# Eight of the weight sums of a down projection: accumulating DMA, or a plain load and an add on GpSimd

## The chip, the cores and the metric

The kernel runs on one core of one Trainium2 chip. The metric is the device time of one execution in microseconds. Before the change it is 768.64 us, the median of three runs (767.77 to 768.9).

## The reference

One layer of a hybrid decoder: 512 tokens of width 1024 go through a state-space mixer and an attention mixer, an output projection, and then a gated MLP with a short convolution. All is float32. What matters here is the last product of the MLP, with D_FF = 2816:

```python
def conv_gated_mlp(x, w_up, conv_w, conv_b, w_down):
    h = x @ w_up.astype(x.dtype)
    h = causal_depthwise_conv(h, conv_w, conv_b)
    gate, val = jnp.split(h, 2, axis=-1)
    return (jax.nn.silu(gate) * val) @ w_down.astype(x.dtype)
...
        hf = rms_norm(x, norm_ffn_w[layer])
        x = x + conv_gated_mlp(hf, w_up[layer], ffn_conv_w[layer], ffn_conv_b[layer], w_down[layer]).astype(x.dtype)
```

## The kernel before

Float32 products are made of three matmuls each: both operands are split into a high part (a cast on ScalarE, `wh`, `oh`) and a low part (the rest, a subtraction on VectorE, `wl`, `ol`), and high x high, high x low and low x high are summed in PSUM (`mm3`, L110).

The down projection is the last stage, from about 650 us on. It cuts the tokens, the inner dimension and the output columns in halves and needs seven products instead of eight (`PRODUCTS`, n = 0 to 6). Their left operands are quarters or sums of quarters of the activations, their right operands quarters of `w_down` or sums of them:

- products 0 and 1 use the quarters B11 and B21 as they are, loaded by SP into `wraw` (`load_unit`);
- products 2, 3, 4 use a running sum T: B11 + B12, then B22 added, then B21 added;
- products 5 and 6 use T again, loaded afresh with B22, then B12 added.

Each quarter has 11 blocks of 128 rows, and a product walks through them in six units of two blocks (1024 columns; the sixth has one block, 512). T[u] is the sum for unit u: six tiles. Where a row names tiles, T[0] and T[1] are both printed as `T`, T[2] to T[5] in the order lists as `T_7091` to `T_7094`.

A unit of a product is worked on so: ScalarE casts T[u] to `wh`, VectorE forms `wl` (both L1218, `split_unit`), TensorE runs 12 matmuls of 512 columns (6 in the last unit). There are three buffers for `wh` and `wl`, so a split can run at most three units ahead of TensorE. In the same loop `next_sum(n, u)` starts the next term of T[u], `SUMS` lets VectorE make sums of activations (L1413, L1419), `split_into` splits the next left operand (L1354 on ScalarE, L1355 on VectorE), and at the end of a product VectorE adds its PSUM banks to the output in SBUF (L1514, one input in PSUM).

The terms of T come by two kinds of DMA. `fresh` (L1200) is a plain load, issued by SP. `gather` (L1207) is a load that adds to what the tile holds, issued by GpSimd. `next_sum` calls them: in product 1, units 4 and 5, for T[2] to T[5] (B11 fresh, then B12 gathered); in products 2, 3 and 5 one gather per unit, as soon as the unit's `wl` has been made; in product 4 one fresh load per unit. T[0] and T[1] get their first two terms before the stage.

The order on ScalarE and VectorE is pinned by the order of the code (`in_turn`); SP and GpSimd work through their queues in the order that the scheduler gives them, and an instruction that waits holds all behind it. At L1155 and L1156, in the up stage, GpSimd has two multiplications of 512 columns per step, placed behind a chosen instruction of VectorE (`in_shadow`).

Of the kernel before, what the change touches and what calls it, by code (L numbers as in the profile page):

```python
# [8 lines left out]
F32 = mybir.dt.float32  # L9
# [6 lines left out]
P = 128  # L16
# [23 lines left out]
def tile_hybrid_layer(  # L40
# [18 lines left out]
    nc = tc.nc  # L59
    act, dve, pool, pe = nc.scalar, nc.vector, nc.gpsimd, nc.tensor  # L60
# [165 lines left out]
    for k in range(NK):  # L226
        ins = pe.matmul(pdt[:64, :], wdt[:, k, :], xh[:, k, :], start=k == 0, stop=False, skip_group_check=True)
        if k < 2:
            tc.keep_in_program_order(ins)
            keep_busy(64 * (1 - k))  # L230
        ins = pe.matmul(
            pdt[:32, :], wdt[:, k, 0:32], xl[:, k, :], start=False, stop=k == NK - 1, skip_group_check=True
        )
# [564 lines left out]
    B11, B12, B21, B22 = 0, 1, 2, 3  # L798
    ADD, SUB = ALU.add, ALU.subtract
# [32 lines left out]
    turn_of = {}  # L832
# [359 lines left out]
    UNITS = [(k, min(k + 2, NH)) for k in range(0, NH, 2)]  # L1192

    def part(q, u):
        return wdown[q, :, UNITS[u][0] * 512 : UNITS[u][1] * 512]

    T = []

    def fresh(q, u):
        nc.sync.dma_start(T[u], part(q, u))  # L1200
# [5 lines left out]
    def gather(q, u):  # L1206
        nc.gpsimd.dma_start(T[u], part(q, u), accum_op=ALU.add)  # L1207
# [143 lines left out]
    q = NH - 1  # L1351
# [55 lines left out]
    pt_ = ctx.enter_context(tc.tile_pool(name="pt", bufs=1, side="right", reuse_waits="tile"))  # L1407
# [39 lines left out]

    ADDED = {2: B22, 3: B21, 5: B12}

    def next_sum(n, u):  # L1450
        if n == 4:
            fresh(B22, u)
        if n in ADDED:
            gather(ADDED[n], u)
        if n == 1 and u > 3:
            for v in ((2, 3), (4, 5))[u - 4]:
                fresh(B11, v)
                gather(B12, v)

    ops = [a11]  # L1460

    def units_of(n):
# [8 lines left out]
        for u, (lo, hi) in enumerate(UNITS):  # L1471
            early = n == 0 and u < 3
            if not early:
                h, l = split_unit(u, T[u] if quarter is None else load_unit(quarter, u))
            next_sum(n, u)
            if (n, u) in SUMS:
                add, v = SUMS[n, u]
# [151 lines left out]
```

## Time and profile before

| | us |
|---|---|
| median of three runs | 768.64 |
| the profiled execution's own time | 770.09 |
| its span, first to last instruction | 768.3 |
| TensorE busy | 759.0 |
| VectorE busy | 600.0 |
| ScalarE busy | 489.0 |
| GpSimd busy | 201.0 |

The granted clock of TensorE is 1.000 over the span. The rows of the profile are read so: start or place, busy time, engine (PE is TensorE, DVE VectorE, ACT ScalarE, POOL GpSimd, SPq SyncE's queue), line, operation, tile written <- tiles read, shapes, count; in brackets, how long the engine sat idle before it and who released it. What GpSimd waited for longest in the down stage (engine, line, tile <- releaser: total, times, longest):

```profile
POOL T L1207 <- DVE wl L1218: 26.0, 10, 13.0
POOL T L1207 <- PE X L110: 20.3, 1, 20.3
POOL T L1207 <- DVE x L1514: 8.3, 3, 3.2
```

A wait is put down to the releaser that came last by the profile; where that engine had long been done, it was another, often a DMA.

### The profile page before, as it was taken

How to read it: one execution, taken by the hardware profiler on the slowest of the kernel's cores; microseconds unless marked ns; L12 is line 12 of the kernel's file. 1: busy time of each engine (PE TensorE's matmuls, PEld its weight loads, DVE VectorE, ACT ScalarE, POOL GpSimd, SP SyncE). 2: the span in 40 equal slices, each digit the busy share in tenths (PEclk: the TensorE clock that was granted, in tenths of full speed). 3: DMA queues.
4: the chain of work that ended last, by engine and by line, in shares of the span. 5: the costliest groups of instructions: out<-in, count | busy, mean ns of one | idle time of the engine just before them, and what ended most of it. 6: DMA issues, size and time to landing. Idle time of an engine off the chain costs nothing.

```text
span 768.3 us, 12543 instructions
## 1 busy us (share of the span) xinstructions
PE 759.0 (99%) x4647; PEld 652.2 (85%) x4647; DVE 600.0 (78%) x965; ACT 489.0 (64%) x870; POOL 201.0 (26%) x250
## 2 busy tenths in 40 slices
PE   9999999999999999999999999999999999999997
PEld 7888878888888768887777799999999999887786
DVE  5896788578567675578794887988888888998785
ACT  7655767754578667785673665666666666665461
POOL 0001013443454542314200001333333333223120
PEclk9999999999999999999999999999999999999999
DMA  9534233143155143343222318888888888589983
GB/s 341 175 105 142 84 123 121 57 137 110 57 164 165 43 137 90 116 138 110 83 83 89 106 57 162 195 196 202 195 198 196 189 194 195 144 227 204 241 180 100
DMA packets 35005, 112.39 MB, mean 146 GB/s; under 512 B 4160, under 2 KB 5248, under 8 KB 34944
## 3 DMA queue, kind: packets, MB, share of 16 engines
q1 hardware_dynamic: 24176, 74.89, 28.7%
q0 software_dynamic: 10336, 36.18, 26.2%
q8 instruction: 36, 0.59, 0.3%
q10 hardware_dynamic: 432, 0.52, 0.2%
q14 instruction: 25, 0.20, 0.1%
HBM read 105.71 MB, written 2.20 MB: 140 GB/s over the span
## 4 chain that ended last, share of the span: by engine, by line
PE 92%; issue 3%; DMA 1%; POOL 1%; DVE 1%; ACT 0%; DVEq 0%; POOLq 0%; ACTq 0%
PE G L110 19%; PE pw L110 17%; PE g L110 13%; PE po L110 12%; PE Z L110 10%; PE Y L110 3%; PE o L684 3%; PE X L110 2%; PE pT L674 2%; PE y L501 2%; DMA T<-in_wdown_dram 1%; PE j L110 1%; PE S L652 1%; PE S L651 1%; POOL T L1207 1%
## 5 line engine op out<-in xcount | busy, mean ns | idle before, releaser
L110 PE MATMUL pw<-wl,xh 128*128 128x512 f32 x192 | 75.9, 395 | 0.0
L110 PE MATMUL pw<-wh,xh 128*128 128x512 f32 x192 | 75.3, 397 | 0.0
L110 PE MATMUL pw<-wh,xl 128*128 128x512 f32 x192 | 75.3, 394 | 0.0
L110 PE MATMUL G<-uh,wh 128*128 128x256 f32 x264 | 72.6, 277 | 0.4 <-ACT wh L923 0.4
L110 PE MATMUL G<-uh,wl 128*128 128x256 f32 x264 | 71.6, 277 | 1.1 <-DVE wl L923 1.1
L110 PE MATMUL G<-ul,wh 128*128 128x256 f32 x264 | 72.5, 276 | 0.0
L97 DVE TENSOR_TENSOR wl<-wraw,wh 128x1024 fp32r<-128x1024 f32 x51 | 63.2, 1241 | 9.3 <-ACT wh L96 9.1
L96 ACT CAST wh<-wraw 128x1024 fp32r<-128x1024 f32 x51 | 53.9, 1056 | 14.7 <-PE g L110 5.3
L110 PE MATMUL g<-xl,wh 128*128 128x512 f32 x144 | 56.7, 394 | 0.0
L110 PE MATMUL g<-xh,wh 128*128 128x512 f32 x144 | 56.5, 393 | 0.0
L110 PE MATMUL g<-xh,wl 128*128 128x512 f32 x144 | 56.5, 393 | 0.0
L968 POOL DMA_DIRECT2D Ta<-in_wup_dram x30 | 26.2, 873 | 113.1 <-DVE wl L923 113.1
L1218 ACT CAST wh<-T 128x1024 fp32r<-128x1024 f32 (+1 forms) x32 | 31.5, 985 | 35.5 <-DMA T<-in_wdown_dram 19.2
L657 ACT ACTIVATE prob<-prob,nm 128x128 f32<-128x128 f32 (+1 forms) x64 | 35.8, 561 | 25.9 <-DVE nm L653 25.8
L923 DVE TENSOR_TENSOR wl<-Ta,wh 128x1024 fp32r<-128x1024 f32 x40 | 48.7, 1218 | 2.6 <-ACT wh L923 2.6
L653 DVE CUSTOM_DVE_ANT_0 prob<-S,prob 128x128 f32<-128x128 f32 (+1 forms) x64 | 30.1, 487 | 26.3 <-PE S L652 23.8
L110 PEld LDWEIGHTS G<-uh,wh 128*128 128x128 f32 x264 | 49.6, 188 | 0.8 <-ACT wh L923 0.8
L110 PEld LDWEIGHTS G<-uh,wl 128*128 128x128 f32 x264 | 48.9, 188 | 1.3 <-DVE wl L923 1.3
L110 PEld LDWEIGHTS G<-ul,wh 128*128 128x128 f32 x264 | 49.6, 188 | 0.0
L1218 DVE TENSOR_TENSOR wl<-T,wh 128x1024 fp32r<-128x1024 f32 (+1 forms) x32 | 36.5, 1139 | 14.8 <-ACT wh L1218 14.6
L923 ACT CAST wh<-Ta 128x1024 fp32r<-128x1024 f32 x40 | 42.1, 1052 | 6.2 <-DMA Ta<-in_wup_dram 4.2
L110 PE MATMUL G<-sh,wh 128*128 128x256 f32 x160 | 44.2, 276 | 0.0
(296 smaller groups left out, 2416.9 us busy)
## 6 DMA issues: line engine op xcount, KB each, us to landing
Ta<-in_wup_dram POOLq DMA_DIRECT2D x30, 512.0 KB, 5.4
T<-in_wdown_dram POOLq DMA_DIRECT2D x20, 512.0 KB, 7.3
wraw<-in_wqk_dram SPq DMA_DIRECT2D x16, 512.0 KB, 3.6
wraw<-in_wout_dram SPq DMA_DIRECT2D x16, 512.0 KB, 3.4
wraw<-in_wup_dram SPq DMA_DIRECT2D x14, 512.0 KB, 4.5
wraw<-in_wxbc_dram SPq DMA_DIRECT2D x11, 512.0 KB, 3.4
Ta<-in_wup_dram SPq DMA_DIRECT2D x10, 512.0 KB, 6.8
Tb<-in_wup_dram SPq DMA_DIRECT2D x10, 512.0 KB, 6.4
```

The lines of the kernel that those rows point to most:

```text
L96: act.copy(h, r)
L97: dve.tensor_tensor(out=l, in0=r, in1=raw(h), op=ALU.subtract)
L110: ins = pe.matmul(o, a, b, start=start and n == 0, stop=stop and n == 2, **kw)
L501: ins = pe.matmul(o[rows, j * P : (j + 1) * P], w[:, h * HD : (h + 1) * HD], m[:, h, :], start=start and j == 0, stop=stop and j == 3, ski ...
L651: pe.matmul(sps[:, :n], qst, ks[:, 0, :n], start=True, stop=False)
L653: dve.tensor_tensor_reduce(out=p, in0=sps[:, :n], in1=p, scale=-1.0, scalar=-NEG, op0=ALU.add, op1=ALU.min, accum_out=nm[:, qb : qb + 1],)
L657: act.activation(p, p, AF.Exp, scale=-1.0, bias=nm[:, qb : qb + 1], accum_out=sm[:, qb : qb + 1])
L674: pe.transpose(t[:, w : w + P], prob[:, o : o + P], ident)
L684: ins = pe.matmul(o[rows, kb * P :], v[:, kb, (2 * pair + i) % 8, :], pt[:, w : w + SEQ - kb * P], start=kb == 0, stop=kb == NTB - 1, skip ...
L923: ordered(act.copy(h, r), lambda: dve.tensor_tensor(out=l, in0=r, in1=raw(h), op=SUB))
L968: last_more[0] = nc.gpsimd.dma_start(t, wup[quarter, q], accum_op=ALU.add)
L1218: ordered(act.copy(hs, src[:, :n]), lambda: dve.tensor_tensor(out=ls, in0=src[:, :n], in1=raw(hs), op=SUB))
```

## The change

Eight of the terms that `gather` brought are now brought by a plain load of SP into a tile of its own (`beside`, four buffers of 1024 columns), and GpSimd adds that tile to T[u] with a `tensor_tensor`. They are B12 for T[3] and T[5] in product 1, and B22 and B21 for T[0], T[2] and T[4] in products 2 and 3. The load is made to wait for the low part that VectorE formed last at that point of the code. The other terms stay gathers.

```diff
     ADDED = {2: B22, 3: B21, 5: B12}
 
+
+    BESIDE_FIRST = (3, 5)
+    BESIDE = (0, 2, 4)
+
+    def add_beside(q, u):
+        w = (UNITS[u][1] - UNITS[u][0]) * 512
+        t = pt_.tile([P, 1024], F32, tag="beside", name="beside", bufs=4)
+        dep = mybir.DependencyInfo(mybir.DependencyClass.Sync, mybir.DependencyReason.DATA)
+        ins = nc.sync.dma_start(t[:, :w], part(q, u))
+        tc.add_manual_dep(ins.ins, turn_of["l"].ins.name, dep, reason="issue_after")
+        pool.tensor_tensor(out=T[u][:, :w], in0=T[u][:, :w], in1=t[:, :w], op=ADD)
+
     def next_sum(n, u):
         if n == 4:
             fresh(B22, u)
-        if n in ADDED:
+        if n in (2, 3) and u in BESIDE:
+            add_beside(ADDED[n], u)
+        elif n in ADDED:
             gather(ADDED[n], u)
         if n == 1 and u > 3:
             for v in ((2, 3), (4, 5))[u - 4]:
                 fresh(B11, v)
-                gather(B12, v)
+                (add_beside if v in BESIDE_FIRST else gather)(B12, v)
```

The instructions of TensorE, VectorE and ScalarE stand in the same order as before. GpSimd's queue, from its last multiplication of the up stage to T[4]'s first gather of the stage and the terms of product 2; before:

```order
L1156 TENSOR_TENSOR KK<-ua 128x512
L1207 DMA T_7091<-in_wdown_dram 128x1024
L1207 DMA T_7092<-in_wdown_dram 128x1024
L1207 DMA T_7093<-in_wdown_dram 128x1024
L1207 DMA T_7094<-in_wdown_dram 128x512
L1207 DMA T<-in_wdown_dram 128x1024 x2
```

and after the change, through product 2's terms:

```order
L1156 TENSOR_TENSOR KK<-ua 128x512
L1207 DMA T_7091<-in_wdown_dram 128x1024
L1207 DMA T_7093<-in_wdown_dram 128x1024
L1460 TENSOR_TENSOR T_7092<-T_7092,beside 128x1024
L1207 DMA T<-in_wdown_dram 128x1024
L1460 TENSOR_TENSOR T_7094<-T_7094,beside 128x512
L1460 TENSOR_TENSOR T<-T,beside 128x1024
L1207 DMA T_7092<-in_wdown_dram 128x1024
L1460 TENSOR_TENSOR T_7091<-T_7091,beside 128x1024
L1207 DMA T_7094<-in_wdown_dram 128x512
L1460 TENSOR_TENSOR T_7093<-T_7093,beside 128x1024
```

T[4]'s gather moved up past T[3]'s term, and gathers and adds now alternate. The rest of the queue goes on so for product 3: the add to T[0], the gathers of T[1] and T[3], the add to T[2], the gather of T[5], the add to T[4].

SP's queue, from the fresh load of T[5] in product 1 to the first fresh load of product 4, as a difference (`out_dram` is the output of product 1):

```order
 L1200 DMA T_7094<-in_wdown_dram 128x512
-L1518 DMA out_dram<-x_85 128x512 x2
+L1458 DMA beside<-in_wdown_dram 128x1024
+L1458 DMA beside<-in_wdown_dram 128x512
+L1458 DMA beside<-in_wdown_dram 128x1024
+L1532 DMA out_dram<-x_85 128x512 x2
+L1458 DMA beside<-in_wdown_dram 128x1024 x5
 L1200 DMA T<-in_wdown_dram 128x1024 x2
```

Three of the new loads (T[3], T[5], and T[0] of product 2) stand ahead of the two stores, five between them and product 4's fresh loads.

## The prediction

> **What bounds the kernel now.** I read the page first, then TensorE's rows in the down stage, then what its waits lead back to.
>
> ```profile
> PE 759.0 (99%) x4647; PEld 652.2 (85%) x4647; DVE 600.0 (78%) x965; ACT 489.0 (64%) x870; POOL 201.0 (26%) x250
> 700.05 0.39 PE L110 MATMUL Y<-wh,oh 128*128 128x512 f32 x1
> 716.24 0.39 PE L110 MATMUL X<-wh,oxh 128*128 128x512 f32 x1
> 733.81 0.39 PE L110 MATMUL Z<-wh,oh 128*128 128x512 f32 x1
> 748.77 0.39 PE L110 MATMUL Y<-wh,oh 128*128 128x512 f32 x1
> ```
>
> TensorE is busy 99% of the span, so only its gaps can be won. The four matmul rows are the first ones of products 3, 4, 5 and 6 of the down stage, each of 66 matmuls. Product 5 takes 748.77 - 733.81 = 14.96 us undisturbed; product 3 takes 16.19 and product 4 takes 17.57. So the two lose 1.23 + 2.61 = **3.8 us**. What ends the largest gap is seen on three engines:
>
> ```profile
> 727.45 1.05 ACT L1218 CAST wh<-T 128x1024 fp32r<-128x1024 f32 x1 [2.30 <-DMA T<-in_wdown_dram]
> 728.53 1.23 DVE L1218 TENSOR_TENSOR wl<-T,wh 128x1024 fp32r<-128x1024 f32 x1 [1.43 <-ACT wh L1218]
> 729.81 0.50 PE L110 MATMUL X<-wl,oxh 128*128 128x512 f32 x1 [0.76 <-DVE wl L1218]
> ```
>
> The sum T lands late, ScalarE casts it, VectorE forms the low part, and TensorE starts at once. Why does T land late? The first row is the DMA view's of 696 to 704 us, the second its of 678 to 682 us (packets, MB, share of the engines); then two of GpSimd's issues, and the first one's time to landing:
>
> ```profile
> q0 software_dynamic: 445, 1.63, 105.6%
> q1 hardware_dynamic: 465, 1.48, 95.3%
> 690.87 0.86 POOL L1207 DMA_DIRECT2D T<-in_wdown_dram x1 [1.59 <-DVE wl L1218]
> 698.48 0.87 POOL L1207 DMA_DIRECT2D T<-in_wdown_dram x1 [1.56 <-DVE ol L1355]
> T<-in_wdown_dram POOLq DMA_DIRECT2D x1, 512.0 KB, 7.3
> ```
>
> Gathers alone fill all 16 DMA engines: 1.63 MB in 8 us, or 2.57 us for one of 0.524 MB; plain loads move 1.48 MB in 4 us, or 1.41 us for one. The gather of 690.87 lands 7.3 us later, at 698.2, and the third one after it is issued 0.3 us behind that, as if no more than three could be under way. So what limits products 3 and 4 is the gathers' DMA time.
>
> **What the change removes.** Eight gathers (7.5 full ones, since unit 5 is half) become plain loads: 7.5 x (2.57 - 1.41) = 8.7 us less DMA time between about 681 and 724 us. The gaps are far smaller than that, so this removes the whole **3.8 us** if nothing else is late. The next candidate on DMA is the gather of T[2] for product 2. Its landing is just in time now:
>
> ```profile
> 688.21 1.05 ACT L1218 CAST wh<-T 128x1024 fp32r<-128x1024 f32 x1 [2.46 <-DMA T<-in_wdown_dram]
> 690.70 0.40 PE L110 MATMUL Z<-wl,oh 128*128 128x512 f32 x1
> ```
>
> From cast to matmul lie 2.49 us, of which 1.05 + 1.23 are the two conversions: 0.2 us to spare. In the changed kernel the plain loads of units 3 and 5 share the engines with this gather, while the gather of T[3] behind it is gone. Bounds: nothing, and the plain loads' whole 1.5 x 1.41 = 2.1 us less the spare, 1.9; I take **0.5 us**, nearer to nothing because a gather of 2.57 us leaves.
>
> **What it adds: SP.** Eight loads in SP's queue, each waiting for the low part of its unit.
>
> ```profile
> T<-in_wdown_dram SPq DMA_DIRECT2D x10, 512.0 KB, 7.0
> ```
>
> Behind the third load stand the two stores of product 1's output, behind the last the fresh loads of product 4; both wait for later work of VectorE than the loads ahead of them do. A load lands in 7.0 us (median of such loads of T), an add takes 2.3, and between a unit's low part and the cast of its next sum lies about one product, 14.96 us. I cost this at nothing; the cover is the 5 us that are left, and each us beyond them would stall TensorE by one.
>
> **What it adds: GpSimd.** Seven adds of 1024 columns and one of 512. The nearest rows:
>
> ```profile
> 620.10 1.29 POOL L1155 TENSOR_TENSOR ua<-ua 128x512 f32<-128x512 f32 x1 [1.75 <-DVE wl L923]
> 621.36 1.29 POOL L1156 TENSOR_TENSOR KK<-ua 128x512 f32<-128x512 f32 x1
> 183.64 1.26 POOL L543 TENSOR_TENSOR yt<-yt 128x256 f32<-128x256 f32 x2
> ```
>
> The first two are 1.26 us apart for 512 columns. The third is a pair of 256 and 128 columns (the loop at L543) in 1.26 us. With a fixed part a and b per column, a + 512b = 2a + 384b = 1.26, so a = 0.25, b = 1.97 ns, and 1024 columns take 2.27 us: 7 x 2.27 + 1.26 = **17.2 us**. GpSimd has the room: its 13 issues between 686 and 724 us take 11.3 us (last row below), and more than half of them go. In its queue T[1]'s gather stands behind T[3]'s add, and later each gather behind one or two adds, so an add that waits for its load holds a gather back. The larger price is elsewhere:
>
> ```profile
> 117.39 1.09 POOL L486 TENSOR_SCALAR_AFFINE_SELECT sc<-sc 128x1024 f32<-128x1024 f32 x1 [7.23 <-ACT ce L484]
> 194.57 1.70 POOL L486 TENSOR_SCALAR_AFFINE_SELECT sc<-sc 128x1024 f32<-128x1024 f32 x1
> 194.11 1.22 DVE L485 TENSOR_TENSOR ce<-ce,cT 128x1024 f32<-128x1024 f32 x1
> 195.24 1.58 DVE L541 TENSOR_TENSOR msl<-y,msh 128x512 fp32r<-128x512 f32 x1
> 656.17 2.36 DVE L1218 TENSOR_TENSOR wl<-wraw,wh 128x1024 fp32r<-128x1024 f32 x2 [0.27 <-ACT wh L1218]
> 657.55 2.15 POOL L1155 TENSOR_TENSOR ua<-ua 128x512 f32<-128x512 f32 x1 [3.59 <-DVE wl L1218]
> 659.66 1.29 POOL L1156 TENSOR_TENSOR KK<-ua 128x512 f32<-128x512 f32 x1
> 660.58 1.45 DVE L1218 TENSOR_TENSOR wl<-wraw,wh 128x1024 fp32r<-128x1024 f32 x1
> 620.34 2.98 DVE L1118 SCALAR_TENSOR_TENSOR ua<-Z,pc,ua 128x511 f32<-128x511 f32 x4 [0.39 <-ACT ua L1111]
> 125.35 0.68 DVE L541 TENSOR_TENSOR msl<-y,msh 128x512 fp32r<-128x512 f32 x1
> 125.96 0.68 DVE L448 SCALAR_TENSOR_TENSOR gz<-th,gz 128x512 f32<-128x512 f32 x1
> 125.38 2.40 POOL L543 TENSOR_TENSOR yt<-yt 128x256 f32<-128x256 f32 x2
> ```
>
> Read in pairs. L486 takes 1.09 us alone, but 1.70 when it meets a VectorE operation with two SBUF inputs: it waits until that ends at 195.3. Then VectorE's L541, 0.68 us elsewhere, takes 1.58: it waits until L486 ends at 196.3. The add at 657.55 likewise takes 2.15, not 1.29, because VectorE's low parts run until 658.5; and the low part at 660.58 takes 1.45, not 1.22, until the add ends at 660.95. So a GpSimd operation and a VectorE operation with two SBUF inputs **exclude each other**, each for the other's whole length. Operations with an input in PSUM show no such stretch: the four at 620.34, beside two adds, take 2.98 us together, and the adds 1.29 each. Who goes first differs: at 195.24 and 660.58 GpSimd went ahead of VectorE's next operation, while at 125.96 VectorE's next one went ahead of the add issued at 125.38 (the pair took 2.40 us, not 1.26). Now VectorE's work in the stretch with the adds, 686 to 724 us:
>
> ```profile
> L1218 DVE TENSOR_TENSOR wl<-T,wh 128x1024 fp32r<-128x1024 f32 (+1 forms) x14 | 16.1, 1148 | 6.0 <-ACT wh L1218 5.9
> L1355 DVE TENSOR_TENSOR ol<-sum,oh 128x512 fp32r<-128x512 f32 (+1 forms) x9 | 5.6, 625 | 0.0
> L1413 DVE TENSOR_TENSOR sum<-sum,KK 128x512 f32<-128x512 f32 (+1 forms) x6 | 3.8, 640 | 0.0
> L1514 DVE TENSOR_TENSOR x<-x,Z 128x512 f32<-128x512 f32 x2 | 1.3, 680 | 0.0
> core 0: us, PE busy (x) PEld busy (x) DVE busy (x) ACT busy (x) POOL busy (x), PEclk, DMA share, GB/s
> 686.00:724.00 38.00, 37.08 (x161) 29.50 (x160) 31.56 (x42) 19.44 (x27) 11.30 (x13) 1.00 1.03 206
> ```
>
> In the last row VectorE's busy time is 31.6 us. All of it has two SBUF inputs except the output adds of L1514, which read PSUM: three pairs of 1.3, less the overlap of starts, 3.7 us. That leaves 27.9 us that must not coincide with the adds. Together 27.9 + 17.2 = 45.1 us. By 724 us TensorE had lost part of its 3.8 us: product 3's 1.23 and the first gap of product 4.
>
> ```profile
> 721.68 0.39 PE L110 MATMUL X<-wh,oxh 128*128 128x512 f32 x1
> 722.45 0.50 PE L110 MATMUL X<-wl,oxh 128*128 128x512 f32 x1 [0.38 <-DVE wl L1218]
> ```
>
> With 14.96 / 66 = 0.23 us from one matmul to the next, this gap is 0.77 - 0.23, and 0.11 more for the stalled matmul's longer row: 0.65. So 1.9 us were lost, and without gaps the same work would be due in 38 - 1.9 = 36.1 us. **45.1 - 36.1 = 9.0 us** too much. VectorE has nothing in hand at the start: T[2]'s low part ends 0.2 us before its matmul. TensorE's queue follows VectorE, so I put these 9.0 us on the path.
>
> I take it that the two alternate, as two of the three places show. [...]
>
> **Sum.** -3.8 + 0.5 + 9.0 = +5.7 us. The profiled execution took 770.09 us (span 768.3), the median is 768.64; on the median this gives **774.3 us**.
>
> **Rivals.**
> *The adds fit in VectorE's pauses.* Its 14 low parts waited 5.9 us for ScalarE, and free time is 36.1 - 27.9 = 8.2 us. If an add held VectorE for less than 8.2 / 17.2 = 48% of its length, nothing would be late and the 3.8 us are won: 764.8 us. For it: the pauses are there. Against it: at 195.24 VectorE's operation can have begun only at 195.24 + 1.58 - 0.68 = 196.14, 0.13 us before L486 ended, so it was held nearly to the end.
> *Both cancel.* If an add held VectorE for about 70% of its length, (8.2 + 3.8) / 17.2, the loss equals the gain: 768.6 us. For it: adds may run beside the six output adds; against it, these are already in the free time.
> *VectorE keeps its turn.* If VectorE's queued operations go first, as at 125.96, an add starts only in a pause, its sum is late, and the gathers that stand behind it in GpSimd's queue are late too, above all T[1]'s gather behind T[0]'s add of product 3. TensorE then waits for sums; VectorE's pauses while it waits are lost. One late gather costs its 7.3 us to landing less the 3 to 4 us that its split runs ahead; once, it adds about 3 us: 777.5 us. For it one row, against it two.
> That the change does not do what it says I leave out: the order lists show the eight loads and adds.
>
> **How the numbers follow.** The forecast gets 0.52, with 2.27 us per add and 0 to 1.9 for T[2] as bounds: 771.5 to 776.5. VectorE first gets 0.26, up to 780. Cancelling gets 0.10, pauses 0.12. The range 766.5 to 779.5 leaves out the pauses' case and the far end of the third. A measurement tells about 0.2%, 1.5 us: faster 0.12, same 0.10, slower 0.78.
>
> **What would show it.** Right: VectorE's low parts (L1218) between 686 and 724 us have means well above 1.15 us, some over 3 us; GpSimd's adds at 2.3 us and up; the casts no longer wait for the DMA; product 2, undisturbed now, loses a few us; products 2 to 4 together lose 8 to 11 us; DMA share falls below 0.9. Wrong: low parts of 1.22 us beside running adds, which would give the first rival; or casts that wait for GpSimd for long while VectorE's rows stay short, which would give the third.

## The result, and the profile after the change

| | before | after |
|---|---|---|
| median, us (four runs of each, side by side) | 768.26 (767.77 to 768.9) | 776.5 (775.08 to 776.88) |
| after / before, 95% interval | | 1.0102 [1.009, 1.0115] |
| the profiled execution's own time | 770.09 | 775.08 |
| its span | 768.3 | 773.3 |
| mean granted clock of TensorE | 1.000 | 0.997 |

The change costs about 1%: 8.2 us between the medians, 7.8 by the ratio. The two profiled executions lie only 5.0 us apart: that of before took longer than any timed run of its kernel, that of after less than the three others. This matters below.

From the page after the change, the busy line, the line of the gathers' queue and the first line of the chain of work that ended last:

```profile
PE 759.4 (98%) x4647; PEld 652.4 (84%) x4647; DVE 612.7 (79%) x965; ACT 489.5 (63%) x870; POOL 218.1 (28%) x250
...
q0 software_dynamic: 9184, 32.25, 23.6%
...
PE 91%; DVE 6%; issue 1%; DMA 0%; ACT 0%; SPq 0%; DVEq 0%; ACTq 0%
```

The gathers' queue moves 32.25 MB where it moved 36.18: the eight terms of 7.5 x 0.524 MB are gone from it. GpSimd is busy 17.1 us longer with as many instructions (eight adds for eight issues of gathers), and VectorE, whose 965 instructions are the same, 12.7 us longer. The chain, which led over the DMA and GpSimd for 1% each, now leads over VectorE for 6%. The shares do not say where that is. The first matmuls of products 2, 3, 4 and 5 of the down stage (TensorE's timeline):

```profile
683.27 0.39 PE L110 MATMUL Z<-wh,oh 128*128 128x512 f32 x1
...
702.97 0.40 PE L110 MATMUL Y<-wh,oh 128*128 128x512 f32 x1
...
722.45 0.39 PE L110 MATMUL X<-wh,oxh 128*128 128x512 f32 x1
...
738.82 0.39 PE L110 MATMUL Z<-wh,oh 128*128 128x512 f32 x1
```

Products 2 to 4 now take 738.82 - 683.27 = 55.55 us. Undisturbed they take 46.05, the stretch from 683.92 to 729.97 us in the run with fills below, where TensorE has no gap: three times 14.96 and the five matmuls of product 1 (5 x 0.23) that stand behind product 2's first one. So they lose 9.50 us: product 2 3.6, product 3 4.5, product 4 1.4. In the profile of before the same stretch, from 683.90 to 733.81, loses 3.86. Where the 9.5 us go, on TensorE's timeline:

```profile
690.95 0.50 PE L110 MATMUL Z<-wl,oh 128*128 128x512 f32 x1 [0.71 <-DVE wl L1218]
...
695.96 0.50 PE L110 MATMUL Z<-wl,oh 128*128 128x512 f32 x1 [1.98 <-DVE wl L1218]
...
711.65 0.80 PE L110 MATMUL Y<-wl,oh 128*128 128x512 f32 x1 [2.73 <-DVE wl L1218]
712.24 0.63 PE L110 MATMUL Y<-wh,ol 128*128 128x512 f32 x1
712.67 0.63 PE L110 MATMUL Y<-wh,oh 128*128 128x512 f32 x1
...
729.39 0.50 PE L110 MATMUL X<-wl,oxh 128*128 128x512 f32 x1 [1.11 <-DVE wl L1218]
```

Every gap is ended by a low part of VectorE. Behind the longest, matmuls follow one another at 0.43 us, not 0.23, until 714.4: about 1.5 of the 9.5 us are a lowered clock (the windows below show 0.66 there). What VectorE does ahead of the gaps, and GpSimd beside it (their timelines):

```profile
687.93 1.83 DVE L1355 TENSOR_TENSOR ol<-sum,oh 128x512 fp32r<-128x512 f32 x1
...
692.50 3.40 DVE L1218 TENSOR_TENSOR wl<-T,wh 128x1024 fp32r<-128x1024 f32 x1
...
704.26 1.21 DVE L1218 TENSOR_TENSOR wl<-T,wh 128x1024 fp32r<-128x1024 f32 x1
...
708.21 3.38 DVE L1218 TENSOR_TENSOR wl<-T,wh 128x1024 fp32r<-128x1024 f32 x1
...
723.78 2.63 DVE L1413 TENSOR_TENSOR sum<-sum,KK 128x256 f32<-128x256 f32 x1
```

```profile
686.81 2.40 POOL L1460 TENSOR_TENSOR T<-T,beside 128x1024 f32<-128x1024 f32 x1 [2.96 <-DMA beside<-in_wdown_dram]
...
690.10 4.73 POOL L1460 TENSOR_TENSOR T<-T,beside 128x512 f32<-128x512 f32 x2
...
703.67 6.84 POOL L1460 TENSOR_TENSOR T<-T,beside 128x1024 f32<-128x1024 f32 x2 [0.74 <-DMA beside<-in_wdown_dram]
```

The low part of 708.21 would take 1.22 us; it takes 3.38, for the pair of adds from 703.67 ends at 710.51 and the low part 1.1 us after that. The sum of 723.78 has 256 columns, 0.42 us elsewhere, and takes 2.63 beside an add from 723.12 to 726.12. An add that begins while VectorE works on PSUM data (686.81) takes 2.40, and that work, the two output adds of 686.74, 1.28 together. Eight VectorE rows of the stretch are so lengthened, one for each add: by 1.15, 1.09, 2.18, 2.21, 1.02, 2.16, 1.21 and 2.21 us, 13.2 us together. The group of low parts in 686 to 724 us (count, then busy time and mean ns, then idle time ahead), and the windows:

```profile
L1218 DVE TENSOR_TENSOR wl<-T,wh 128x1024 fp32r<-128x1024 f32 (+1 forms) x13 | 20.3, 1558 | 1.3 <-ACT wh L1218 1.3
```

```profile
686.00:724.00 38.00, 32.56 (x133) 25.43 (x132) 36.72 (x36) 18.58 (x26) 24.99 (x14) 0.96 0.75 186
...
710.00:715.00 5.00, 3.35 (x9) 2.69 (x10) 5.00 (x6) 0.34 (x1) 1.98 (x3) 0.66 0.59 94
```

VectorE (third busy time) has no pause but 1.3 us, with 36 instructions where it made 42 before; the DMA share is 0.75 where it was 1.03. ScalarE's casts hardly wait for transfers any more (total, times, longest):

```profile
ACT wh L1218 <- DMA T<-in_wdown_dram: 3.2, 2, 2.4
```

Before it was 19.2 us in 12 waits. The relief that the loads bring is there, and the adds take it back and more.

### The profile page after: what moved, and what is told of

Same layout as the page of the kernel before. It is cut to its first block, busy times and chain, and to the rows that moved or that the text cites. A ratio compares the mean times of both kernels' runs of the same rounds, so it can differ in the third digit from the quotient of the medians.

```text
span 773.3 us, 12548 instructions
## 1 busy us (share of the span) xinstructions
PE 759.4 (98%) x4647; PEld 652.4 (84%) x4647; DVE 612.7 (79%) x965; ACT 489.5 (63%) x870; POOL 218.1 (28%) x250
## 3 DMA queue, kind: packets, MB, share of 16 engines
q0 software_dynamic: 9184, 32.25, 23.6%
## 4 chain that ended last, share of the span: by engine, by line
PE 91%; DVE 6%; issue 1%; DMA 0%; ACT 0%; SPq 0%; DVEq 0%; ACTq 0%
PE G L110 19%; PE pw L110 17%; PE g L110 13%; PE po L110 11%; PE Z L110 10%; PE Y L110 4%; PE o L684 3%; DVE wl L1218 2%; PE X L110 2%; PE pT L674 2%; PE y L501 2%; PE j L110 1%; PE S L652 1%; PE S L651 1%; DVE x L1528 1%
## 5 line engine op out<-in xcount | busy, mean ns | idle before, releaser
L1218 DVE TENSOR_TENSOR wl<-T,wh 128x1024 fp32r<-128x1024 f32 (+1 forms) x32 | 41.8, 1306 | 8.2 <-ACT wh L1218 8.2
```

The costliest lines, as they stand in the source:

```text
L1218: ordered(act.copy(hs, src[:, :n]), lambda: dve.tensor_tensor(out=ls, in0=src[:, :n], in1=raw(hs), op=SUB))
```

## The experiments

The theory: an add on GpSimd and an operation of VectorE with two SBUF inputs exclude each other, and VectorE has not enough pauses for the adds. The rivals: the adds make the sums late, or hold the gathers behind them in GpSimd's queue; or the plain loads themselves cost. Each run is timed beside the kernel before on the same chip. The last column is what products 2 to 4 lose in that run's profile, from the first matmul of product 2 to that of product 5 less 46.05 us.

| run | median, us | ratio to before, 95% interval | loss, us |
|---|---|---|---|
| the change again | 776.14 | 1.0091 [1.0076, 1.0107] | 9.0 |
| loads, no adds | 767.28 | 0.9976 [0.9966, 0.9986] | 0.2 |
| fills instead of adds | 766.36 | 0.9975 [0.994, 1.0009] | 0.0 |
| copies instead of adds | 767.23 | 0.9987 [0.9974, 0.9999] | 0.5 |
| adds in halves | 775.49 | 1.0104 [1.0076, 1.0131] | 8.1 |
| three adds on GpSimd | 770.96 | 1.0039 [1.0025, 1.0053] | 3.8 |
| eight adds on VectorE | 770.27 | 1.0016 [1.0001, 1.0032] | 3.5 |
| three adds on VectorE | 770.3 | 1.0036 [1.0019, 1.0053] | 6.1 |
| four, placed later | 771.29 | 1.0043 [1.0026, 1.0059] | 4.8 |
| three, placed later | 767.63 | 0.9989 [0.998, 0.9999] | 1.3 |
| the kernel before, again | 768.88 | 1.0009 [0.9998, 1.0019] | 2.5 |

### The change again, its adds left out, and its adds turned into fills

The first run is the changed kernel as it is.

> The changed kernel as it is, once more. Theories: (A) GpSimd's adds and VectorE's operations with two SBUF inputs exclude each other, and the time lost is VectorE's; (B) the sums come late because load, add and gather stand in one queue of GpSimd; (C) the plain loads themselves are in the way of other transfers. All expect about 776.5 us against 768.3 before. The two profiled executions so far differ by 5.0 us where the medians differ by 8.2; if that is chance of one execution, this profile comes out nearer 776.5 with the same VectorE rows (six or more of the 128x512 and 128x1024 operations stretched by 1 to 2.2 us), and TensorE's slow clock after a gap of about 3 us (0.66 in 710 to 715 us) shows again.

The time is the change's own again, 776.14 us, with gaps of 0.59, 2.00, 0.31, 0.95, 0.30 and 1.43 us, all ended by low parts, and VectorE rows of 3.40, 3.42 and 3.39 us. Which operation meets which add differs between the two executions, the total less: 9.0 us lost here, 9.50 there.

Without the adds:

```diff
-        pool.tensor_tensor(out=T[u][:, :w], in0=T[u][:, :w], in1=t[:, :w], op=ADD)
```

> The eight loads stay, the eight adds are left out, so eight terms of the weight sums are missing from what is computed. (A) and (B): the 3.8 us of the late gathers are won and nothing is added, 764 to 766 us. (C): the loads still cost, 774 us or more.

And with two fills in the place of each add, which write the same tiles in the same place of GpSimd's queue, but read nothing:

```diff
-        pool.tensor_tensor(out=T[u][:, :w], in0=T[u][:, :w], in1=t[:, :w], op=ADD)
+        first = pool.memset(t[:, :w], 0.0)
+        then = pool.memset(T[u][:, :w], 0.0)
```

> Each add is replaced by two memsets of GpSimd, one on the tile beside and one on the sum, in the same place of its queue, waiting for the same load, and with the same reader waiting for them; the weight sums are lost by it. GpSimd is held for about as long (estimate 2 us, if a memset of 1024 columns takes about 1), but reads nothing from SBUF. (A) with the reading as the shared part: no VectorE row is stretched, 764 to 767 us. (A) with writing shared too: stretched rows again, 772 us or more. (B): 773 us or more without stretched VectorE rows. (C): 773 us or more.

Without adds 767.28 us, 1.3 more than the 766 at most that were expected, with fills 766.36, and no gap of TensorE in the stage in either. The fills' rows on GpSimd, then the low parts of the same run in 686 to 724 us:

```profile
692.42 0.96 POOL L1460 MEMSET beside<- 128x1024 f32 x1 [1.91 <-DMA beside<-in_wdown_dram]
693.32 0.95 POOL L1461 MEMSET T<- 128x1024 f32 x1
694.22 0.87 POOL L1207 DMA_DIRECT2D T<-in_wdown_dram  x1
```

```profile
L1218 DVE TENSOR_TENSOR wl<-T,wh 128x1024 fp32r<-128x1024 f32 (+1 forms) x16 | 18.5, 1156 | 3.5 <-ACT wh L1218 3.4
```

The fills are there, wait for the loads, keep their place ahead of the gathers, and take 1.9 us for each pair, and no low part is longer for it: mean 1156 ns, where the run without adds has 1154. So late sums and GpSimd's queue are refuted as the cause, for that queue held the same places with 1.9 us in each where an add takes 2.4, and the loads are refuted by both runs. The cost goes with GpSimd's reads: the fills write the tile of the sum as the adds do, and read nothing.

The two runs also size both terms of the sum. Loads without adds are worth 0.24%, 1.8 us; the adds cost 1.0091 - 0.9976 = 1.15%, **8.8 us**.

### One input instead of two

```diff
-        pool.tensor_tensor(out=T[u][:, :w], in0=T[u][:, :w], in1=t[:, :w], op=ADD)
+        pool.tensor_copy(out=T[u][:, :w], in_=t[:, :w])
```

> The changed kernel, but GpSimd copies the tile beside into T[u] in place of adding it: one input read from SBUF instead of two; the eight sums are lost. If any read of SBUF by GpSimd excludes VectorE, low parts (L1218) beside a copy are as long as 1.22 us plus what is left of the copy, and their mean in the stage is clearly over 1.15 us; the time then goes by the copies' length: 7.5 x 1.0 to 1.9 us = 7.5 to 14 us against 7.4 us that VectorE has free, 767 to 773 us. If only an operation with two SBUF inputs does, all low parts stay at 1.22 and the time is that of the kernel without adds, 766 to 768.

767.23 us, and still the copies exclude. GpSimd's timeline, then VectorE's:

```profile
693.21 1.04 POOL L1460 COPY T<-beside 128x1024 f32<-128x1024 f32 x1 [3.61 <-DMA beside<-in_wdown_dram]
...
698.36 1.49 POOL L1460 COPY T<-beside 128x1024 f32<-128x1024 f32 x1 [3.30 <-DMA beside<-in_wdown_dram]
...
711.30 4.08 POOL L1460 COPY T<-beside 128x1024 f32<-128x1024 f32 x1 [1.76 <-DMA beside<-in_wdown_dram]
```

```profile
697.74 1.22 DVE L1218 TENSOR_TENSOR wl<-T,wh 128x1024 fp32r<-128x1024 f32 x1
698.87 1.53 DVE L1413 TENSOR_TENSOR sum<-sum,KK 128x512 f32<-128x512 f32 x1
...
713.79 0.68 DVE L1355 TENSOR_TENSOR ol<-sum,oh 128x512 fp32r<-128x512 f32 x1
715.06 1.39 DVE L1218 TENSOR_TENSOR wl<-T,wh 128x1024 fp32r<-128x1024 f32 x1 [0.59 <-ACT wh L1218]
```

A copy takes 1.04 us alone. The one of 698.36 waits until the low part ends at 698.96, and the sum behind it takes 1.53 us, not 0.68. The one of 711.30 takes 4.08 us: VectorE's operations stand back to back until 714.47, and it gets in only at their end. So one input from SBUF is enough, and here VectorE kept its turn for 3 us. The expectation had looked for it in the low parts, whose mean stayed at 1155 ns; it was in the sums of L1413 (mean 1058 ns against 640 without adds). Seven copies of 1.04 and one of 0.61 are 7.9 us, near the 7.4 us that VectorE had free, and TensorE loses half a microsecond.

### The length of one hold

```diff
-        pool.tensor_tensor(out=T[u][:, :w], in0=T[u][:, :w], in1=t[:, :w], op=ADD)
+        for c in range(0, w, 512):
+            pool.tensor_tensor(out=T[u][:, c : c + 512], in0=T[u][:, c : c + 512], in1=t[:, c : c + 512], op=ADD)
```

> The changed kernel, but each of the seven adds of 1024 columns on GpSimd is made as two of 512; the same sums. If only the total length of the adds counts, 7.5 x 2 x 1.26 = 18.9 us against 7.5 x 2.40 = 18.0: 776 to 778 us. If it is the length of one hold that counts (VectorE rows of 3.4 us, a gap of 2.7 us on TensorE and the lowered clock behind it), no VectorE row of 1024 columns is over about 2.6 us, the clock stays at 1.00, and the time is 1.5 to 3 us below the changed kernel's: 773 to 775. If VectorE slips in between the halves, so that the halves wait, T is late and casts wait for GpSimd: over 778.

775.49 us. No VectorE row is over 2.32 us, no gap of TensorE over 1.51, and the clock stays at 1.00 in 686 to 724 us, as the second expectation has it (VectorE's longest row, then TensorE's longest gap):

```profile
694.77 2.32 DVE L1218 TENSOR_TENSOR wl<-T,wh 128x1024 fp32r<-128x1024 f32 x1
```

```profile
709.97 0.50 PE L110 MATMUL Y<-wl,oh 128*128 128x512 f32 x1 [1.51 <-DVE wl L1218]
```

But the median lies between the two times that were expected, and the ratio's interval, 1.0076 to 1.0131, reaches over the change's own, so no gain can be told. Fifteen adds of 1.30 us are 19.5 us in place of 18.1, which may have taken what the quiet clock gave; that is not shown. Shown is that shorter holds alone do not bring back the 8 us.

### Fewer adds, and adds on VectorE

Eight adds on VectorE, two or three units behind the loads:

```diff
-        pool.tensor_tensor(out=T[u][:, :w], in0=T[u][:, :w], in1=t[:, :w], op=ADD)
+        due.setdefault(LATER[at], []).append((u, w, t))
...
+    def add_due(n, u):
+        for v, w, t in due.pop((n, u), ()):
+            in_turn("l", dve.tensor_tensor(out=T[v][:, :w], in0=T[v][:, :w], in1=t[:, :w], op=ADD))
```

> The eight adds are made by VectorE, two or three units after the load was issued. They take it 7 x 1.14 + 0.6 = 8.6 us instead of being kept out for 17.2. (A): 27.9 + 8.6 = 36.5 us of work where 36.1 are free, so about 0.4 us too much and the 3.8 won: 765 to 767 us, faster than before. (B): GpSimd's queue holds gathers alone, 765 us. (C): 773 us or more.

770.27 us, a miss by 3 us or more. The window of that run and that of the run without adds:

```profile
686.00:724.00 38.00, 36.26 (x155) 28.36 (x153) 38.00 (x49) 20.93 (x29) 5.22 (x6) 1.00 0.87 222
```

```profile
686.00:724.00 38.00, 38.00 (x169) 31.24 (x168) 34.34 (x47) 22.17 (x31) 5.21 (x6) 1.00 0.91 238
```

VectorE is busy 38.00 of 38 us. Without adds, at TensorE's full pace, it had 3.66 us free; eight adds of about 1.13 us (one of them half) are 8.5. That is 4.8 us too much, and 3.5 are lost. An add costs VectorE 1.13 us there and 13.2 / 7.5 = 1.8 us when GpSimd makes it.

So three terms were left beside, three adds (`BESIDE = {2: (0,), 3: (2, 4)}`, none in product 1), on either engine:

> Only three terms go beside and are added by GpSimd (B22 of T[0] in product 2, B21 of T[2] and T[4] in product 3), the other five are gathers again; the same sums. Budget theory: in the kernel without adds VectorE is busy 34.3 of 38 us in 686 to 724, 3.7 of these with PSUM inputs, so 7.4 us are free for adds; three adds of 2.40 take 7.2 and just fit, and 3 x 1.16 = 3.5 us of DMA time go: TensorE loses 0 to 2 us in products 2 to 4, 765 to 768 us. Rival, each add costs its share whatever the room: (776.1 - 767.3) / 7.5 = 1.2 us for each, 3 x 1.2 over the kernel without adds, 770 to 772 us.

> The same three terms beside, added by VectorE between its own operations, at units (2,4), (3,5) and (4,1); the same sums. In the run with all eight adds on VectorE that engine was busy 38.0 of 38 us: 7.5 x 1.13 = 8.5 us against 3.7 free, 4.8 too much, and the span was 3.4 us over that without adds. Three adds take 3.4 us of the 3.7. Budget theory: 765 to 767 us, 2 to 4 us below the kernel before, with VectorE nearly full and no gap of TensorE over 0.5 us. If landing of the remaining gathers still sets the pace, casts wait for the DMA as before and the time is 767.5 to 769.

770.96 and 770.3 us: the budget theory missed both. The budget fits and still TensorE loses 3.8 and 6.1 us in these profiles. On VectorE in the run with three adds on GpSimd, and in the run with three adds on VectorE:

```profile
714.54 2.60 DVE L1218 TENSOR_TENSOR wl<-T,wh 128x1024 fp32r<-128x1024 f32 x1 [2.23 <-ACT wh L1218]
...
719.15 2.63 DVE L1413 TENSOR_TENSOR sum<-sum,KK 128x256 f32<-128x256 f32 x1
```

```profile
720.64 1.23 DVE L1462 TENSOR_TENSOR T<-T,beside 128x1024 f32<-128x1024 f32 x1 [1.61 <-DMA beside<-in_wdown_dram]
```

In the first, VectorE is idle for 2.23 us, since a cast waits for a gather, and then an add holds just the low part that TensorE needs: its free time was not where the adds fell. In the second, an add waits 1.61 us for its load, all of VectorE's queue waits behind it, and TensorE has a gap of 1.89 us at 725.19 with the lowered clock behind it (0.66 in 725 to 730 us). The profiled execution of the second took 773.2 us, 2.9 more than the median of its kernel, so an ordinary one can lose only about 3, and whether it has this gap is not seen. The first time lies where its rival put it, but that an add costs its share whatever the room is not shown by that: the rows give these other reasons, and five of the terms are gathers again.

Two more kernels put the adds later. Four (`BESIDE_FIRST = (5,)`, `BESIDE = {2: (2,), 3: (0, 4)}`):

> Four terms beside (B12 of T[5] in product 1, B22 of T[2] in product 2, B21 of T[0] and T[4] in product 3), added by VectorE at units (2,3), (3,0), (3,4) and (4,2), a product's third or more after their loads are asked for, so that no add waits for its load; the other four terms are gathers; the same sums. VectorE pays 3 x 1.13 + 0.6 = 4.0 us against 3.7 free, DMA saves 3.5 x 1.16 = 4.1 us. If the two misses with adds on VectorE came of a full engine (eight adds) and of an add that waited 1.6 us for its load (three adds), this one is at 766.5 to 768, at or a little below the kernel before. If gathers that share the DMA engines with loads from SP land later whatever is saved, it is at 768.5 to 771.

771.29 us. That no add would wait for its load was wrong:

```profile
702.24 1.23 DVE L1462 TENSOR_TENSOR T<-T,beside 128x1024 f32<-128x1024 f32 x1 [1.97 <-DMA beside<-in_wdown_dram]
```

That load took 10.9 us to land among the gathers, and the wait became TensorE's gap of 1.87 us at 705.86. The three others without it (`BESIDE = {2: (), 3: (0, 4)}`):

> As the run with four terms on VectorE, without the one whose add waited 1.97 us for its load (B22 of T[2], a load that took 10.9 us to land beside the gathers): B12 of T[5], B21 of T[0] and T[4] stay beside, added by VectorE at (2,3), (3,4) and (4,2), the other five terms are gathers; the same sums. That add's wait ended in the gap of 1.87 us at 705.86 and its end in the lowered clock; without it about 771.3 - 2 to 3 = 768 to 769 us, level with the kernel before. If the saving of 2.5 x 1.16 = 2.9 us of DMA time also shows in the gaps of product 4, 766.5 to 768. If any mixing of plain loads with gathers costs, 769.5 or more.

767.63 us, ratio 0.9989 [0.998, 0.9999]; in its profile, of 768.64 us, no gap of TensorE is ended by another engine and 1.3 us are lost. So mixing plain loads with gathers need not cost. Taking out the one term whose add waited brought 3.7 us. This kernel is below the change for certain and below the kernel before by 0.1%, which is less than the 0.2% that such a measurement tells with confidence.

### The kernel before, again

> The kernel before, unchanged, to see what products 3 and 4 of the down stage lose in another execution. The prediction's first term, 3.8 us, is from one profiled execution of 770.09 us, 1.5 to 1.8 over the medians of the kernel before. If that execution lost more than most, this profile, where its time is at 768.0 to 768.8, loses 1.5 to 3 us there, and the loss and the time go together. If the 3.8 us are the kernel's usual loss, they are found again, and what the loads alone won, 0.24% or 1.9 us, fell short of it for another reason.

The first matmuls of products 2 and 5 in its profile, of 769.25 us:

```profile
684.48 0.39 PE L110 MATMUL Z<-wh,oh 128*128 128x512 f32 x1
...
733.01 0.39 PE L110 MATMUL Z<-wh,oh 128*128 128x512 f32 x1
```

48.53 us, a loss of 2.5 us where the profile of 770.09 us lost 3.9. It is 0.9 us above the median of its neighbours, so the expectation's 768.0 to 768.8 was not met and a median execution itself is still not seen; but in these two the loss falls with the time, and the 1.8 us that the loads alone won fit an execution that loses about 2.

## Why the prediction was right, and where it was off

The sign, the mechanism and the range were right; the predicted time, 774.3, is 2.2 us below 776.5.

**What the change removes: mis-sized.** The prediction took 3.8 us from the gaps of one execution, less 0.5 for T[2], and added them to the median of others. The loads without adds measured 1.8 us. The gaps vary between executions, 3.9 and 2.5 us in two profiles, and the prediction read them in a long one. In that execution they could all be won: 770.09 - 3.8 = 766.3 us, and the profiled execution of the loads without adds took 766.86. So the sum should have stood on that execution's own time: 770.09 + 5.7 = 775.8 us, where the changed kernel's profiled execution took 775.08 and its median is 776.5. Within the pair of profiles the sum held almost exactly: 9.50 - 3.86 = +5.6 us, predicted +5.7 (the whole executions lie 5.0 apart, since product 2 began 0.63 us earlier).

**T[2]'s gather, +0.5: not found in the changed kernel.** Its cast stood 4.31 us behind product 2's first matmul (688.21 and 683.90) and stands 4.28 behind it now (687.55 and 683.27). Product 2's first gap, 0.71 us, is an exclusion: the low part begins 1.1 us after its cast has ended, behind the row of 687.93.

**SP's loads at nothing: right** (the run without adds has no gap).

**GpSimd's adds: 2.27 us predicted, 2.40 measured,** 18.1 us in all instead of 17.2.

**The exclusion, +9.0: right in size, 8.8 by the runs.** Its composition was partly another. Of 18.1 us of adds VectorE was held for 13.2, 73%; the rest fell on its work with PSUM data or in pauses. Some 1.5 us of the loss in the profile fall on the lowered clock behind a long gap, which the prediction did not have; whether they come on top is not shown, for the adds in halves, without it, lose 8.1 us. And the prediction reckoned with 8.2 us free on VectorE; the run without adds shows 3.66 us of pauses and 3.7 of PSUM work, 7.4 us. With 18.1 and 7.4 us its own reckoning gives 10.7, so that 9.0 lies so near to 8.8 is in part luck.

**The rivals.** "The adds fit" did not come. "Both cancel" did not either, though its condition, an add that holds VectorE for about 70% of its length, was all but met with 73%: it set the hold against 8.2 us of free time, 3.7 of which are PSUM work, which an add did not lengthen (the pair of output adds of 686.74 took 1.28 us beside one, and 1.27 in the run with four adds on VectorE). Against the pauses alone 13.2 - 3.66 = 9.5 us are left, what TensorE loses. "VectorE keeps its turn" did not set this time: no cast of 684 to 739 us has a wait that GpSimd ended, and TensorE waits for low parts, not for sums. But the behaviour exists, as the copy of 4.08 us shows. In the changed kernel GpSimd got in between two queued operations of VectorE (the low part of 708.21 waits for the second add of the pair, which was issued while others ran). But the first add of that pair, issued at 703.67, took 4.07 us, while VectorE made the low part of 704.26 in its usual 1.21, and in the run with copies one waited for 3 us. What decides it is open.

**What it said would show it.** Low parts' mean 1558 ns, two rows over 3 us, adds from 2.39 us up, no casts that wait for the DMA but two, DMA share 0.75, products 2 to 4 losing 9.5 us of the 8 to 11: all found.

## What to carry to other kernels

A job moved to an engine with room is not free if its operations and those of the engine that is full exclude each other (here eight adds cost 8.8 us): count, in the stage itself, the busy time of both that must not coincide, and ask also whether the free time lies where the new work falls, since three adds that fitted on average still cost about 3 us. A gain that is read from the gaps of one profiled execution belongs to that execution's own time; before it is put on a median, a second profile shows whether the gaps are the same. Where the order on an engine is pinned, as VectorE's is here, an add must stand far enough behind its load: one term whose add waited 1.97 us cost 3.7 us.

## What the runs showed of the hardware that was not expected

TensorE's clock fell behind gaps of 1.87 to 2.73 us, and not each time. In the run with four adds placed later it fell only some time after the gap (TensorE's timeline):

```profile
705.86 0.50 PE L110 MATMUL Y<-wl,oh 128*128 128x512 f32 x1 [1.87 <-DVE wl L1218]
...
707.12 0.53 PE L110 MATMUL Y<-wh,oh 128*128 128x512 f32 x1
707.45 0.63 PE L110 MATMUL Y<-wl,oh 128*128 128x512 f32 x1
...
710.77 0.40 PE L110 MATMUL Y<-wh,oh 128*128 128x512 f32 x1
```

In the change the granted clock was 0.90 in 711.00 to 711.25 us, 0.50 from there to 714.50 and 0.77 in 714.50 to 714.75, so it stood at half for about 3.4 us. Six gaps of TensorE, the granted clock of a stretch of 5 us that begins in the gap, and the rows behind:

| gap, us | run | granted clock (stretch, us) | matmul steps behind it |
|---|---|---|---|
| 1.84 | three adds on GpSimd | 1.00 (724 to 729) | 0.23 us |
| 1.87 | four, placed later | 0.72 (705 to 710) | 0.43 us, from 1.3 us after the gap |
| 1.89 | three adds on VectorE | 0.66 (725 to 730) | 0.43 us at once |
| 1.98 | the change | 1.00 (695 to 700) | 0.23 us |
| 2.00 | the change again | 0.66 (696 to 701) | 0.42 us at once |
| 2.73 | the change | 0.66 (710 to 715) | 0.43 us at once |

The gap's length alone does not order them: the clock stayed at 1.00 behind 1.98 us and fell behind 1.87 and 1.89. What decides is not shown. Each of the four falls cost about 1.5 us, an estimate from seven or eight steps of 0.43 us in the place of 0.23, not much less than a gap of 1.9.

GpSimd's times here, alone: an add of 128x1024 float32 in SBUF 2.40 us, a copy of one input 1.04, a fill 0.96. Only the fill left VectorE alone: in 686 to 724 us its low parts had a mean of 1156 ns and its sums of L1413 one of 642, without adds 1154 and 640; beside the copies the sums had 1058.
